# Where the factors of the RMS norms are multiplied in: a ten-sublayer kernel on one core

## The chip, the core and the metric

The kernel runs on one core of one Trainium2 chip. The metric is the device time of one execution in microseconds (us), the median of several. The core's engines each work through their own list of instructions in order: TensorE (PE in the profile; its weight loads are PEld), VectorE (DVE), ScalarE (ACT), GpSimd (POOL) and SyncE (SP), which here issues the transfers. An instruction starts when what stands before it on its engine is done and what it reads and writes is ready on the others.

## The reference, cut to what matters

256 tokens of width 1024 pass through ten sublayers, all in float32. Each one normalises its input, computes something from it, normalises the result and adds it to x:

```
def rms_norm(x, w):
    y = x * rsqrt(mean(x * x, -1) + 1e-6)
    return y * w

for l in range(2):
    x = x + 0.5 * rms_norm(swiglu(rms_norm(x, pre0)), post0)        # (l, 0)
    x = x + rms_norm(mixer(rms_norm(x, pre1)), post1)               # (l, 1)
    x = x + rms_norm(cross_attention(rms_norm(x, pre2)), post2)     # (l, 2)
    x = x + 0.5 * rms_norm(swiglu(rms_norm(x, pre3)), post3)        # (l, 3)
x = x + rms_norm(mixer2(rms_norm(x, pre)), post)                    # (2, 0)
x = x + rms_norm(square(relu(rms_norm(x, pre) @ w1)) @ w2, post)    # (2, 1)

swiglu(u) = (silu(u @ w_gate) * (u @ w_up)) @ w_down                # 1024 -> 2816 -> 1024
```

The mean in the norm makes one number per token, called the factor here: x is multiplied by the factor and by a weight per column. The two mixers of the first block hold a gated delta rule, whose triangular systems are solved in levels (the inverse stage below), a retention and a short convolution; `mixer2` has four groups of its own. Their formulas don't matter for what follows.

## The kernel before, in words

x lies in SBUF for the whole time, as two tiles of 128 tokens (tile 0 and 1) in one long table, named `tables` in the rows. All products take their operands as two float32 numbers of reduced length, a high half (h) and a low half (l), and are three matmuls each: high by high, low by high, high by low (`mm3`, at L436). The weights come as units of 512 KB. SP transfers a unit into one of three `raw` buffers, ScalarE casts it to the high half `wh` (L393), and VectorE subtracts to get the low half `wl` (L394; POOL does so for some units). A raw buffer is free for the next transfer when both have read it.

A sublayer boundary, for each token tile, is this chain:

- `post` (L498 to L512): ScalarE squares the two result banks with a running sum (L502), POOL makes the factor in three instructions (the sum of both halves at L504, scale and epsilon at L453, the power -1/2 at L456), VectorE multiplies each bank by factor and weight into `pd` (L510) and adds `pd` to x (L512).
- `normT` (L483 to L496), the pre-norm of the next sublayer: the same Squares on x (L488), the same three POOL instructions (L490, L453, L456), then VectorE makes `u` = x * factor * weight, in two halves of 512 columns (L495).
- `toT`: TensorE transposes `u` into a PSUM bank (L439), ScalarE casts the bank to `xh` (L393) and VectorE subtracts to get `xl` (L394). Now the next sublayer's products can read the tile.

While this chain runs for one tile, TensorE works on the other tile's products where there are any.

A feed-forward sublayer (`ffn`) goes through its 2816 hidden columns in blocks, a first one of 256 (`wh` tiles then hold four of the eight contraction steps of a projection) and five of 512. For each block and token tile: gate product, up product, Silu of the gate (L611), its product with the up result into `hf` (L613), transposes of `hf`, down product into banks that stay for the whole sublayer. The MLP (`mlp`, (2, 1)) has eight blocks of 512 with the Relu of L1924 in their place.

The order of instructions on each engine is not the order of the code. A planner lays the whole program out beforehand on a simulated timeline and fixes one order per engine; a change of some instructions can move others anywhere. At the start, x's first tile comes first, then a 128 x 128 unit matrix, the weight of the first pre-norm, the first weight unit and x's second tile.

## Time and profile before

| | us |
|---|---|
| median of 3 runs | 1839.99 |
| the three runs | 1834.03, 1839.99, 1847.09 |
| the profiled execution: its time | 1836.08 |
| its span in the trace | 1834.0 |

[...] Busy times in the span: TensorE 1768.2 us, its weight loads 1517.9 (they run beside matmuls), VectorE 1077.6, ScalarE 908.2, POOL 201.9. The busy time of an engine is the sum over its instructions without overlap; where a row says `[1.94 <-DVE u L495]`, the engine stood idle for 1.94 us before this instruction, and what it waited for last was `u` of line 495 on VectorE. A row with x2 stands for two instructions one after the other, with the time of both.

### The profile page before, as it was taken

To read this page: it belongs to the slowest core of one execution; us is meant where nothing else is said; L and a number is where in the kernel's file an instruction comes from. 1 tells how busy PE (TensorE), PEld (TensorE's weight loads), DVE (VectorE), ACT (ScalarE), POOL (GpSimd) and SP (SyncE) were. 2 spreads that over 40 slices of the span, in tenths; PEclk is the share of its full clock that TensorE was granted. 3 is DMA by queue.
4 is the path that set the end of the run, shared out by engine and by line. 5 is a ranking of instruction groups with operands and counts; after the bars stand their busy time and mean duration, and the time that the engine had idled before them with its cause. 6 is when DMAs were issued, how large, how long until landed. Compare 5 with 4: busy or idle time off the path is not lost. (4 is left out here: it accounts for less than half of the span.)

```text
span 1834.0 us, 25097 instructions
## 1 busy us (share of the span) xinstructions
PE 1768.2 (96%) x9712; PEld 1517.9 (83%) x9712; DVE 1077.6 (59%) x1544; ACT 908.2 (50%) x1458; POOL 201.9 (11%) x240
## 2 busy tenths in 40 slices
PE   7999999999999999999999999999999899989998
PEld 6888799888988887888789988988888788878886
DVE  5454577765555546555467676546455668465554
ACT  5434565545544445444465464545344676344442
POOL 0000343121000000000133211000000120110000
PEclk9999999999999999999999999999999999599999
DMA  7555432434536664656544332636567532135552
GB/s 250 207 200 198 155 130 76 132 96 146 162 137 197 197 197 143 207 185 202 187 144 138 96 115 84 206 122 205 164 196 219 170 135 76 39 126 173 187 177 84
DMA packets 82775, 287.05 MB, mean 157 GB/s; under 512 B 11104, under 2 KB 12512, under 8 KB 82656
## 3 DMA queue, kind: packets, MB, share of 16 engines
q1 hardware_dynamic: 82656, 285.46, 47.9%
q8 instruction: 76, 1.25, 0.3%
q14 instruction: 43, 0.35, 0.1%
HBM read 284.37 MB, written 1.05 MB: 156 GB/s over the span
## 5 line engine op out<-in xcount | busy, mean ns | idle before, releaser
L394 DVE TENSOR_TENSOR wl<-raw,wh 128x1024 fp32r<-128x1024 f32 x473 | 576.6, 1231 | 361.3 <-ACT wh L393 323.6
L393 ACT CAST wh<-raw 128x1024 fp32r<-128x1024 f32 x505 | 521.1, 1051 | 339.8 <-DMA raw<-in_wst 196.3
L436 PE MATMUL mm<-wh,xh 128*128 128x512 f32 (+1 forms) x1184 | 457.7, 388 | 6.4 <-ACT xh L393 6.1
L436 PE MATMUL mm<-wh,xl 128*128 128x512 f32 (+1 forms) x1184 | 452.5, 385 | 8.7 <-DVE xl L394 8.6
L436 PE MATMUL mm<-wl,xh 128*128 128x512 f32 (+1 forms) x1184 | 453.1, 384 | 0.3 <-DVE wl L394 0.3
L436 PEld LDWEIGHTS mm<-wh,xl 128*128 128x128 f32 x1184 | 225.2, 191 | 55.0 <-DVE xl L394 12.8
L436 PEld LDWEIGHTS mm<-wh,xh 128*128 128x128 f32 x1184 | 226.0, 191 | 51.2 <-ACT xh L393 10.2
L436 PEld LDWEIGHTS mm<-wl,xh 128*128 128x128 f32 x1184 | 225.7, 191 | 41.3 <-DVE wl L394 1.1
L436 PE MATMUL bank<-wh,xh 128*128 128x512 f32 x544 | 213.3, 392 | 4.4 <-ACT xh L393 4.4
L436 PE MATMUL bank<-wl,xh 128*128 128x512 f32 x544 | 213.8, 393 | 0.0
L436 PE MATMUL bank<-wh,xl 128*128 128x512 f32 x544 | 201.7, 390 | 0.0
L436 PE MATMUL mm<-xh,wh 128*128 128x256 f32 x552 | 160.1, 290 | 0.0
L436 PE MATMUL mm<-xh,wl 128*128 128x256 f32 x552 | 158.5, 288 | 0.7 <-DVE wl L394 0.6
L436 PE MATMUL mm<-xl,wh 128*128 128x256 f32 x552 | 158.7, 288 | 0.0
L394 DVE TENSOR_TENSOR xl<-tr,xh 128x512 fp32r<-128x512 f32 (+1 forms) x118 | 77.2, 664 | 108.0 <-ACT xh L393 107.8
L394 POOL TENSOR_TENSOR wl<-raw,wh 128x1024 fp32r<-128x1024 f32 x32 | 84.7, 2649 | 458.5 <-ACT wh L393 451.9
L393 ACT CAST xh<-tr 128x512 fp32r<-128x512 f32 (+1 forms) x118 | 65.9, 565 | 135.3 <-PE tr L439 134.4
L436 PEld LDWEIGHTS bank<-wh,xh 128*128 128x128 f32 x544 | 102.1, 188 | 28.0 <-ACT xh L393 6.4
L436 PEld LDWEIGHTS bank<-wh,xl 128*128 128x128 f32 x544 | 102.2, 188 | 21.1
L436 PEld LDWEIGHTS bank<-wl,xh 128*128 128x128 f32 x544 | 102.2, 188 | 20.5
L436 PEld LDWEIGHTS mm<-xh,wl 128*128 128x128 f32 x552 | 106.7, 194 | 2.2 <-DVE wl L394 1.5
L436 PEld LDWEIGHTS mm<-xh,wh 128*128 128x128 f32 x552 | 106.9, 194 | 1.4 <-issue 0.7
(458 smaller groups left out, 2004.5 us busy)
## 6 DMA issues: line engine op xcount, KB each, us to landing
raw<-in_wst SPq DMA_DIRECT2D x505, 512.0 KB, 4.4
wpre<-in_norm_pre SPq DMA_DIRECT2D x8, 512.0 KB, 6.5
wpost<-in_norm_post SPq DMA_DIRECT2D x8, 512.0 KB, 6.1
mem<-in_mem SPq DMA_DIRECT2D x4, 512.0 KB, 3.4
rel<-in_rel SPq DMA_DIRECT2D x2, 512.0 KB, 4.4
wmem<-in_mem_norm SPq DMA_DIRECT2D x2, 512.0 KB, 3.8
out<-tables SPq DMA_DIRECT2D x4, 256.0 KB, 2.1
abias<-in_abias SPq DMA_DIRECT2D x3, 256.0 KB, 4.1
```

The source lines that it names most:

```text
L393: a = self.nc.scalar.copy(h, raw)
L394: return a, (eng or self.nc.vector).tensor_tensor(out=l, in0=raw, in1=h.bitcast(F32), op=ALU.subtract)
L436: return self.place(self.nc.tensor.matmul(out, a, b, start=start, stop=stop))
```

## The change

The three POOL instructions of a factor become two (`mean_rsqrt`): the scale moves into ScalarE's Squares, sum and epsilon become one instruction, the power stays. In `post`, each bank is multiplied by its weight right behind the Squares, without the factor (`pd`), and factor and addition become one instruction, x = pd * factor + x. In `normT` a norm may be late: then `u` = x * weight without the factor, the transposes follow, and the Squares and the factor come behind them. Since the factor is one number per token, and a product's row belongs to one token, it can be multiplied into the product's result. The late norms are the pre-norms of the four feed-forward sublayers and of the MLP, whose first products are read in one place each: the Silu takes the factor as its scale, `hf` = up * factor * silu; the MLP's Relu takes the factor's square as its scale, r2, made once for each tile. The other five pre-norms multiply the factor in at `u`, as before. `tables` has 32 more columns, for the factors that now live longer.

```diff
+    def mean_rsqrt(self, halves, f, out=None, then=None):
+        ss = self.small(2, "ss")
+        for g in range(2):
+            nc.scalar.activation(self.junk, halves[g], AF.Square, scale=math.sqrt(f / DM), accum_out=ss[:, g:g + 1])
+            if then:
+                then(g)
+        s1 = self.small(1, "s1")
+        nc.gpsimd.tensor_scalar(out=s1, in0=ss[:, 1:2], scalar1=ss[:, 0:1], scalar2=f * EPS, op0=ALU.add, op1=ALU.add)
+        r = self.small(1, "rs") if out is None else out
+        nc.gpsimd.tensor_tensor(out=r, in0=s1, in1=self.mhalf, op=ALU.pow)
+        return r
...
-    def normT(self, src, wb, T, t):
+    def normT(self, src, wb, T, t, late=None):
...
+        if late is None:
+            rs = self.mean_rsqrt(halves, 1.0)
         for g in range(2):
...
-            nc.vector.scalar_tensor_tensor(out=u, in0=src[:, sl], scalar=rs, in1=wb[:, sl], op0=ALU.mult, op1=ALU.mult)
+            if late is None:
+                nc.vector.scalar_tensor_tensor(out=u, in0=halves[g], scalar=rs, in1=w, op0=ALU.mult, op1=ALU.mult)
+            else:
+                nc.vector.tensor_tensor(out=u, in0=halves[g], in1=w, op=ALU.mult)
             self.toT(u, T, g * 4, 4, t)
+        if late is not None:
+            self.mean_rsqrt(halves, 1.0, late)
...
     def post(self, t, banks, wb, half):
...
+        def then(g):
+            d = self.w("pd")
+            nc.vector.tensor_tensor(out=d, in0=banks[g], in1=wb[:, g * 512:g * 512 + 512], op=ALU.mult)
+            ds.append(d)
+        rs = self.mean_rsqrt(banks, 4.0 if half else 1.0, None, then)
         for g in range(2):
-            nc.scalar.activation(self.junk, banks[g], AF.Square, accum_out=ss[:, g:g + 1])
...
-            nc.vector.scalar_tensor_tensor(out=d, in0=banks[g], scalar=rs, in1=wb[:, sl], op0=ALU.mult, op1=ALU.mult)
-            xg = self.x[t][:, sl]
-            nc.vector.tensor_tensor(out=xg, in0=xg, in1=d, op=ALU.add)
+            xg = self.x[t][:, g * 512:g * 512 + 512]
+            nc.vector.scalar_tensor_tensor(out=xg, in0=ds[g], scalar=rs, in1=xg, op0=ALU.mult, op1=ALU.add)
...
-            nc.scalar.activation(s_[:, :fw], pg[:, :fw], AF.Silu)
+            nc.scalar.activation(s_[:, :fw], pg[:, :fw], AF.Silu, scale=rs[t])
             h = self.w("hf")
-            nc.vector.tensor_tensor(out=h[:, :fw], in0=pu[:, :fw], in1=s_[:, :fw], op=ALU.mult)
+            nc.vector.scalar_tensor_tensor(out=h[:, :fw], in0=pu[:, :fw], scalar=rs[t], in1=s_[:, :fw], op0=ALU.mult, op1=ALU.mult)
...
+                if j == 0:
+                    nc.vector.tensor_tensor(out=r2[t], in0=rs[t], in1=rs[t], op=ALU.mult)
                 r_ = self.w("relu")
-                nc.scalar.activation(r_, ps, AF.Relu)
+                nc.scalar.activation(r_, ps, AF.Relu, scale=r2[t])
...
+        late = lambda l, s: (l, s) == (2, 1) or l < 2 and s in (0, 3)
```

The lines of the changed kernel are numbered otherwise: L502 and L488 become one line, L488; L510 becomes L521, L512 becomes L526, `u` without factor is L509, the Silu L625, the square of the factor L1939. How the planner's order moves is shown at three places.

At the start of the program, TensorE, before. Numbers behind a name tell the buffers apart. The bank `mm_237` is the up product of tile 0, whose second half of the contraction reads `xh_109`; `mm_273` is the gate product of tile 1, which reads the second tile's part of `xh_108`.

```order
L436 MATMUL mm_237<-wh_178,xl_110 128x256
L436 MATMUL mm_237<-wh_184,xh_109 128x256
L436 MATMUL mm_273<-wh_103,xh_108 128x256
L436 MATMUL mm_273<-wl_104,xh_108 128x256
L436 MATMUL mm_237<-wl_185,xh_109 128x256
L436 MATMUL mm_237<-wh_184,xl_111 128x256
```

The same place in the change, where the up product is `mm_231` and tile 1's gate product `mm_267`:

```order
L436 MATMUL mm_231<-wh_178,xl_111 128x256
L436 MATMUL mm_231<-wh_178,xh_109 128x256
L436 MATMUL mm_231<-wl_179,xh_109 128x256
L436 MATMUL mm_231<-wh_178,xl_111 128x256
L436 MATMUL mm_267<-wh_103,xh_108 128x256
L436 MATMUL mm_267<-wl_104,xh_108 128x256
```

All twelve matmuls of the up product's second half now stand ahead of tile 1's first gate product; before, eleven of them stood behind its first two.

ScalarE at the same place, before; the last two `xh` casts are those of tile 1, and `sg` is the Silu of tile 0:

```order
L393 CAST wh<-raw 128x1024 x2
L393 CAST rtile<-wab 128x128
L861 ACTIVATE tables<-tables 128x8 x2
L393 CAST wh<-raw 128x1024
L611 ACT_TABLE_LOAD
L611 ACTIVATE sg<-mm 128x256
L393 CAST wh<-raw 128x1024
L393 CAST xh<-tr 128x4x128 x2
L393 CAST wh<-raw 128x1024 x3
L611 ACTIVATE sg<-mm 128x256
```

And in the change, behind the last `xh` cast of tile 0:

```order
L488 ACTIVATE tables,ss<-tables 128x512
L393 CAST wh<-raw 128x1024
L393 CAST xh<-tr 128x4x128
L393 CAST wh<-raw 128x1024
L393 CAST rtile<-wab 128x128
L875 ACTIVATE tables<-tables 128x8 x2
L393 CAST wh<-raw 128x1024
L393 CAST xh<-tr 128x4x128
L393 CAST wh<-raw 128x1024
L625 ACT_TABLE_LOAD
L625 ACTIVATE sg<-mm,tables 128x256
L393 CAST wh<-raw 128x1024 x3
```

The two `xh` casts of tile 1 now stand apart, three weight casts and one weight cast sooner and both ahead of the Silu; the Silu stands behind one more weight cast.

VectorE at the boundary from the second mixer to the MLP, before. `pd<-tr` belongs to tile 0, `pd<-mm` to tile 1:

```order
L394 TENSOR_TENSOR xl<-bank,xh 128x2x128
L510 SCALAR_TENSOR_TENSOR pd<-tr,rs_14666,wpost 128x512 x2
L512 TENSOR_TENSOR tables<-tables,pd 128x512 x2
L495 SCALAR_TENSOR_TENSOR u<-tables,rs_14685,wpre 128x512 x2
L510 SCALAR_TENSOR_TENSOR pd<-mm,rs_14724,wpost 128x512 x2
L394 TENSOR_TENSOR xl<-tr,xh 128x4x128
L512 TENSOR_TENSOR tables<-tables,pd 128x512
L394 TENSOR_TENSOR xl<-tr,xh 128x4x128
L512 TENSOR_TENSOR tables<-tables,pd 128x512
L394 TENSOR_TENSOR wl<-raw,wh 128x1024 x3
```

And in the change:

```order
L521 TENSOR_TENSOR pd<-tr,wpost 128x512 x2
L394 TENSOR_TENSOR xl<-bank,xh 128x2x128
L526 SCALAR_TENSOR_TENSOR tables<-pd,rs,tables 128x512 x2
L509 TENSOR_TENSOR u<-tables,wpre 128x512 x2
L1939 TENSOR_TENSOR tables<-tables 128x1
L521 TENSOR_TENSOR pd<-mm,wpost 128x512 x2
L394 TENSOR_TENSOR xl<-tr,xh 128x4x128
L526 SCALAR_TENSOR_TENSOR tables<-pd,rs,tables 128x512 x2
L394 TENSOR_TENSOR xl<-tr,xh 128x4x128
L509 TENSOR_TENSOR u<-tables,wpre 128x512
L394 TENSOR_TENSOR wl<-raw,wh 128x1024
```

The products with the post weight stand ahead of the `xl` of their surroundings, the additions behind it; `u` of tile 0 follows its x directly, with the square of the factor (L1939) behind it.

VectorE in the inverse stage of the first mixer, before. `P1s` and `X` are the steps of the level chain (L711, L716, which become L725 and L730), `conv` the convolution's steps (L892, which become L906):

```order
L394 TENSOR_TENSOR wl<-raw,wh 128x1024
L711 TENSOR_TENSOR P1s<-P_2467,tables 128x512
L711 TENSOR_TENSOR P1s<-P_2497,tables 128x512
L394 TENSOR_TENSOR wl<-raw,wh 128x1024
L716 TENSOR_TENSOR X<-X,P_2549 128x128x4
L892 SCALAR_TENSOR_TENSOR conv<-st,tables,conv 128x254
L716 TENSOR_TENSOR X<-X,P_2572 128x128x4
```

And in the change:

```order
L725 TENSOR_TENSOR P1s<-P_2483,tables 128x512
L906 SCALAR_TENSOR_TENSOR conv<-st,tables,conv 128x254
L913 SCALAR_TENSOR_TENSOR conv<-th,conv 128x512
L906 SCALAR_TENSOR_TENSOR conv<-st,tables,conv 128x254
L730 TENSOR_TENSOR X<-X,P_2535 128x128x4
L906 SCALAR_TENSOR_TENSOR conv<-st,tables,conv 128x255
L730 TENSOR_TENSOR X<-X,P_2558 128x128x4
```

Steps of the convolution now stand between the steps of the chain where weight splits stood, here and at the same place of the second layer.

## Rows read from the trace of the kernel before

**Rows 1.** Page, busy time of TensorE and the others, share, instructions:

```profile
PE 1768.2 (96%) x9712; PEld 1517.9 (83%) x9712; DVE 1077.6 (59%) x1544; ACT 908.2 (50%) x1458; POOL 201.9 (11%) x240
```

**Rows 2.** TensorE's waits by releaser: total us, number of waits, longest.

```profile
PE tr L439 <- DVE u L495: 19.8, 11, 8.8
PE mm L436 <- DVE xl L394: 8.6, 7, 1.6
PE mm L436 <- ACT xh L393: 6.1, 6, 3.5
```

**Rows 3.** Timeline, second mixer to MLP: start us, us, engine, line, operation, idle before.

```profile
1627.03 0.19 POOL L504 TENSOR_TENSOR s<-ss 128x1 f32<-128x1 f32 x1 [5.51 <-ACT tables L502]
...
1627.59 0.56 POOL L456 TENSOR_TENSOR rs<-rs,tables 128x1 f32<-128x1 f32 x1
...
1628.18 1.41 DVE L510 SCALAR_TENSOR_TENSOR pd<-tr,rs,wpost 128x512 f32<-128x512 f32 x2 [0.51 <-POOL rs L456]
...
1629.51 1.28 DVE L512 TENSOR_TENSOR tables<-tables,pd 128x512 f32<-128x512 f32 x2
...
1630.28 0.63 ACT L488 ACTIVATE tables<-tables 128x512 bf16<-128x512 f32 x1 [3.07 <-DVE tables L512]
...
1632.39 0.56 POOL L456 TENSOR_TENSOR rs<-rs,tables 128x1 f32<-128x1 f32 x1
...
1632.99 1.41 DVE L495 SCALAR_TENSOR_TENSOR u<-tables,rs,wpre 128x512 f32<-128x512 f32 x2 [2.19 <-POOL rs L456]
...
1633.88 1.29 PE L439 MATMUL tr<-tables,u 128*128 128x128 f32 x8 [1.94 <-DVE u L495]
...
1635.12 1.41 DVE L510 SCALAR_TENSOR_TENSOR pd<-mm,rs,wpost 128x512 f32<-128x512 f32 x2 [0.72 <-POOL rs L456]
...
1635.19 0.50 PE L436 MATMUL mm<-wh,xh 128*128 128x512 f32 x1
...
1637.18 0.79 PE L436 MATMUL mm<-wh,xl 128*128 128x512 f32 x1 [1.16 <-DVE xl L394]
```

**Rows 4.** Timelines of ScalarE and of TensorE at the start.

```profile
17.91 1.05 ACT L393 CAST wh<-raw 128x1024 fp32r<-128x1024 f32 x1 [3.21 <-DMA raw<-in_wst]
...
21.88 1.04 ACT L393 CAST wh<-raw 128x1024 fp32r<-128x1024 f32 x1 [1.23 <-DMA raw<-in_wst]
22.84 1.06 ACT L393 CAST xh<-tr 128x512 fp32r<-128x512 f32 x2
...
19.67 0.28 PE L436 MATMUL mm<-wh,xh 128*128 128x256 f32 x1
23.47 0.39 PE L436 MATMUL mm<-wh,xh 128*128 128x256 f32 x1 [3.52 <-ACT xh L393]
```

**Rows 5.** Timeline of the end.

```profile
1828.35 1.41 DVE L510 SCALAR_TENSOR_TENSOR pd<-bank,rs,wpost 128x512 f32<-128x512 f32 x2 [4.48 <-POOL rs L456]
1829.68 1.28 DVE L512 TENSOR_TENSOR tables<-tables,pd 128x512 f32<-128x512 f32 x2
```

**Rows 6.** Windows, busy us (x instructions) of five engines, granted clock, DMA share, GB/s.

```profile
211.00:217.00 6.00, 5.35 (x16) 4.25 (x17) 6.00 (x6) 3.27 (x6) 2.85 (x2) 0.72 0.00 0
...
1635.00:1643.00 8.00, 6.83 (x19) 4.87 (x18) 7.21 (x9) 4.90 (x9) 2.82 (x4) 0.57 0.23 71
1430.00:1446.00 16.00, 11.79 (x53) 8.46 (x53) 14.48 (x37) 11.47 (x20) 4.29 (x7) 1.00 0.37 131
...
1550.00:1610.00 60.00, 56.46 (x280) 50.79 (x279) 34.28 (x85) 21.58 (x57) 7.85 (x10) 0.60 0.12 40
```

**Rows 7.** Groups by line and form: busy us, mean ns of one.

```profile
L495 DVE SCALAR_TENSOR_TENSOR u<-tables,rs,wpre 128x512 f32<-128x512 f32 x40 | 28.3, 748 | 31.2 <-POOL rs L456 31.2
...
L613 DVE TENSOR_TENSOR hf<-mm,sg 128x512 f32<-128x512 f32 x40 | 27.3, 684 | 13.5 <-PE mm L436 13.5
...
L887 ACT ACTIVATE conv<-st,tables 128x256 f32<-128x256 f32 x24 | 12.3, 511 | 0.5
...
L886 ACT COPY st<-mm 128x256 f32<-128x256 f32 x24 | 8.9, 373 | 21.6 <-PE mm L436 19.3 <-issue 2.3
```

More of the change, by code (lines that the diff above doesn't have):

```diff
@@ L287, in __init__ @@
         nc = self.nc
-        self.tables, self.used = self.cst.tile([128, 5744], F32, name="tables"), 0
+        self.tables, self.used = self.cst.tile([128, 5776], F32, name="tables"), 0
         self.x = []
@@ L487, in normT @@
         for g in range(2):
-            nc.scalar.activation(self.junk, src[:, g * 512:g * 512 + 512], AF.Square, accum_out=ss[:, g:g + 1])
+            nc.scalar.activation(self.junk, halves[g], AF.Square, scale=math.sqrt(f / DM), accum_out=ss[:, g:g + 1])
+            if then:
+                then(g)
         s1 = self.small(1, "s1")
-        nc.gpsimd.tensor_tensor(out=s1, in0=ss[:, 0:1], in1=ss[:, 1:2], op=ALU.add)
-        rs = self.rsqrt(s1, 1.0 / DM, EPS)
+        nc.gpsimd.tensor_scalar(out=s1, in0=ss[:, 1:2], scalar1=ss[:, 0:1], scalar2=f * EPS, op0=ALU.add, op1=ALU.add)
@@ L496, in normT @@
             self.toT(u, T, g * 4, 4, t)
+        if late is not None:
+            self.mean_rsqrt(halves, 1.0, late)
     def post(self, t, banks, wb, half):
         nc = self.nc
-        ss = self.small(2, "ss2")
-        for g in range(2):
-            nc.scalar.activation(self.junk, banks[g], AF.Square, accum_out=ss[:, g:g + 1])
-        s1 = self.small(1, "s1")
-        nc.gpsimd.tensor_tensor(out=s1, in0=ss[:, 0:1], in1=ss[:, 1:2], op=ALU.add)
-        f = 4.0 if half else 1.0
-        rs = self.rsqrt(s1, f / DM, f * EPS)
@@ L507, in post @@
-        for g in range(2):
-            d = self.w("pd")
-            sl = slice(g * 512, g * 512 + 512)
-            nc.vector.scalar_tensor_tensor(out=d, in0=banks[g], scalar=rs, in1=wb[:, sl], op0=ALU.mult, op1=ALU.mult)
-            xg = self.x[t][:, sl]
-            nc.vector.tensor_tensor(out=xg, in0=xg, in1=d, op=ALU.add)
+        ds = []
+        def then(g):
+            d = self.w("pd")
+            nc.vector.tensor_tensor(out=d, in0=banks[g], in1=wb[:, g * 512:g * 512 + 512], op=ALU.mult)
+            ds.append(d)
@@ L598, in ffn_plan, with ffn @@
             self.plan((nm + "_down", l, j), fw // 128)
-    def ffn(self, l, s, T, wpost, after):
+    def ffn(self, l, s, T, wpost, after, rs):
         nc = self.nc
@@ L1909, in mlp_plan, with mlp @@
             self.plan(("mlp2", j), 4)
-    def mlp(self, T, wpost, after):
+    def mlp(self, T, wpost, after, rs):
         nc = self.nc
         self.mark("mlp")
+        r2 = [self.tab(1), self.tab(1)]
         accs = [[self.bank() for g in range(2)] for t in range(2)]
@@ L1975, in run @@
         T = self.newT()
+        rs = [self.tab(1), self.tab(1)]
         for t in range(2):
-            self.normT(self.x[t], wp, T, t)
+            self.normT(self.x[t], wp, T, t, rs[t] if late(*subs[0]) else None)
         self.tri = None
@@ L1984, in run @@
                 self.mix2_tables()
-            nT = []
+            nT, nrs = [], [self.tab(1), self.tab(1)]
             bw = {}
@@ L1994, in run, with after @@
             if i + 1 < len(subs):
-                def after(t, bw=bw, nT=nT, nl=subs[i + 1]):
+                def after(t, bw=bw, nT=nT, nl=subs[i + 1], nrs=nrs):
                     if t == 0:
                         nT.extend(self.newT())
-                    self.normT(self.x[t], bw["pre"], nT, t)
+                    self.normT(self.x[t], bw["pre"], nT, t, nrs[t] if late(*nl) else None)
                     if t == (nl in FB):
@@ L2005, in run @@
             if l == 2:
-                (self.mix2 if s == 0 else self.mlp)(T, po, after)
+                if s == 0:
+                    self.mix2(T, po, after)
+                else:
+                    self.mlp(T, po, after, rs)
             elif s == 0 or s == 3:
-                self.ffn(l, 1 if s == 0 else 2, T, po, after)
+                self.ffn(l, 1 if s == 0 else 2, T, po, after, rs)
             elif s == 1:
@@ L2012, in run @@
                 self.xattn(l, T, kv, po, after)
-            T = nT
+            T, rs = nT, nrs
 def kernel(**inputs):
```

4 lines of the change are left out of this document (3 added, 1 removed).

## The prediction

> **What bounds the kernel now.** I read the busy shares first: TensorE is busy for 1768.2 of 1834.0 us and no other engine reaches 60% [rows 1]. So a change can only pay where TensorE stands still or runs at half clock, and the next view is TensorE's list of waits. Its largest entries belong to the norms. Transposes waited for the normalised tile `u` 19.8 us in 11 places, of which one, 8.8 us, is the start of the program; the other ten are sublayer boundaries and make 11.0 us. First products waited 8.6 us in seven places for `xl`, the low half of the transposed tile. They waited 6.1 us for `xh`, the high half, of which 3.5 in one place [rows 2]. Third, the timeline of one boundary (second mixer to MLP, 1626 to 1638 us) shows what lies in these waits: one chain over four engines. The Pool factor (three instructions, 1627.03 to 1628.15), two multiplies and two adds on VectorE (1628.18 to 1630.79), two Squares on ScalarE from 1630.28, a second Pool factor (ready at 1632.95), then `u` at 1632.99; the transposes start at 1633.88 after 1.94 us of idleness. The first products then wait 1.16 us more, because VectorE computes the second token tile's `pd` (1.41 us from 1635.12) before it gets to `xl` [rows 3].
>
> **The change, part by part.** The time of the profiled execution is 1836.1 us, 3.9 under the median of the runs shown; the sum is made against 1836.1.
>
> *Boundary chain.* Pool's first instruction starts 0.56 us before its third (1627.03 and 1627.59); of the two steps in between one goes, so 0.28 us per factor [rows 3]. In `post`, the product with the weight moves ahead of the factor; behind it stand two fused multiply-adds. The nearest row is `u`, which is fused too and reads both its tiles from SBUF: 1.41 us for two, 0.75 one alone [rows 3, 7]. The first half of x is then ready 0.75 us after the factor. Now it takes until 1630.2, which is 2.0 us, since both multiplies run before the first add [rows 3]. The second weight product waits behind the second Square of its bank and behind `xl` work on VectorE; I take 0.3 us back for that. An ordinary boundary chain is thus 0.28 + 1.25 + 0.28 - 0.3 = 1.5 us shorter. Where the following norm is a late one, `u` follows x at once: two fused operations (1.41) and a plain product (0.68, [rows 7]), 2.1 us after the factor. Now this is 1628.15 to 1633.75, 5.6 us [rows 3]. So 5.6 - 2.1 + 0.28 - 0.3 = 3.5 us shorter.
>
> *(a) Waits for u, 11.0 us in ten places.* Their mean is 1.1 us, below 1.5; the 1.94 stands at a late place, below 3.5. For the first token tile they should vanish. For the second tile the chain starts only after TensorE's last product, and TensorE arrives sooner by what it has gained before. I leave 2.0 us there and take **9.0** (bounds: half, 5.0; all, 11.0).
>
> *(b) Waits for xl, 8.6 us in seven places.* VectorE's row order now has the weight products before `xl` and the adds behind it, as the quoted VectorE rows show. `xl` then follows `xh` by one operation of 0.68 us, of which the two products with `xh` that come first (0.50 the one at 1635.19) cover most [rows 3]. The mean of the seven is 1.2 us; I count on five of them at 1.0 each, less 0.2 where the products have 256 columns and cover less, and leave two to weight splits that may still stand ahead: **4.8** (bounds: half of that, 2.5, and seven at 1.0, 7.0).
>
> *(c) The start.* ScalarE's queue holds a weight cast that waits 1.23 us for its transfer until 21.88; behind it stand the two `xh` casts of the second token tile, and TensorE waits 3.52 us for them [rows 4]. In the new order, as quoted, one of these casts stands ahead of the weight cast of 17.91, the other right behind it: both done at 17.91 + 1.05 + 0.53 = 19.5. TensorE asks for them later than now, when it comes to a stop behind the product of 19.67: the twelve products of the up product's second half now stand first [rows 4]. So the 3.52 us go. But the Silu now stands behind the late weight cast, and what hangs on it may come late; I take 0.5 back: **3.0** (bounds 0, if that cast binds again, and 3.5).
>
> *(d) The end.* The last two multiplies and adds take from 1828.35 to 1830.96 [rows 5]; two fused operations take 1.41, so 1.20, and one Pool instruction, 0.28: **1.5** (bounds 1.2 and 1.5).
>
> *(e) The clock.* Behind three boundaries the granted clock is 0.72 over 6 us twice (211 to 217 and 918 to 924, of which the first is shown) and 0.57 over 8 us: 1.7 + 1.7 + 3.4 = 6.8 us lost, since at half clock a product takes twice as long. Another boundary had 4.2 us of idle in 16 and stayed at 1.00 [rows 6], so idleness alone does not decide. I take a little over a third, **2.5** (bounds 0 and 6.8). [...]
>
> *What is added.* 48 Silus and 16 Relus get their scale as a per-token column. The nearest rows are the convolution's activation with two such columns (511 ns) and a copy of the same shape (373 ns) [rows 7]: 0.07 us per column, 4.5 us of ScalarE in all. [...] The 48 `hf` products become fused ones, 0.75 for 0.68, 3 us of VectorE. Two 128x1 squares of the factor come in the MLP. The late Squares and their factor now run behind `u`; the Silu that reads the factor comes a whole projection later. All of it costs nothing on the path, because ScalarE is half idle and waits for TensorE before these; without that cover at most 7.5 us would come back.
>
> Sum: 9.0 + 4.8 + 3.0 + 1.5 + 2.5 = **20.8 us**, bounds 8.7 and 29.8. 1836.1 - 20.8 = 1815.3; from the median, 1819.2. I say **1817 us**.
>
> **The rivals.**
>
> *Half of it turns into another wait (21%).* At some boundaries ScalarE's order keeps a weight cast, which waits for a transfer, ahead of the second tile's Square or of its `xh`. For this speaks the start, where exactly such a cast held TensorE [rows 4]; against it, that the transfers are released by VectorE's splits, which come earlier too. Then (a) gives 5, (b) 4, (c) 0, (d) 1.5, (e) 0: 10.5 us, 1826.
>
> *The clock holds as well (13%).* All of (e), and the upper ends of (a) and (b) in part: 25 to 30 us, 1808. The half-clock stretches behind boundaries speak for it [rows 6], the 16 us stretch against.
>
> *The planner's new order loses the clock in the two first mixers (9%).* The change makes the scheduler lay out the whole program anew; in both layers' inverse stage, convolutions move between the steps of the level chain, as quoted. What such a stage can cost shows the later mixer's: granted clock 0.60 over 60 us with TensorE busy for 56.5, so 24 us lost [rows 6]. If both layers fell that far, 48 - 20.8 = 27 us slower than now, 1863. A loss of 20.8 cancels the gain, so one layer alone; slower by over 1% it is from 43 (1858.4 - 1836.1 + 20.8). Against it: TensorE's rows in these stages are the same products, and it did not wait there.
>
> *It does not do what it says (8%).* The factor is needed anyway; if Silu, Relu or VectorE's square waits for the late one, the wait only moves. In the MLP's place, as quoted, that square stands ahead of the second tile's weight products. The late factor takes half of x (0.75) and the stretch from the first Square to the end of Pool (1630.28 to 1632.95, 2.67) less the dropped step (0.28): 3.1 us behind the post factor, against 2.8 for both `u` (1.41 + 2 x 0.68). So VectorE stands for 0.3 us at one place [rows 3]; this smallness speaks against it; a ScalarE that comes late to those Squares would speak for it. Time: 1836.
>
> **How the numbers follow.** The forecast has 49%. A measurement of this kernel can tell about 1% from no change: under 1821.6 is faster, over 1858.4 slower, from the median of 1840.0. The forecast's own spread, by its bounds, puts 39 of its 49 under 1821.6. Faster: 39 + 13 + 2 of the first rival = 54%. Same: 10 + 19 + 8 = 37%. Slower: 9%. For the range I go from 1836.1 - 29.8, and a few us of spread between executions (the runs shown differ by 13 us), to the case with nothing gained from the profile's side: 1801 to 1834.
>
> **What would show it.** In the profile of the changed kernel the waits of transposes for `u` without the start should fall from 11.0 to about 2 us; the products' waits for `xl` from 8.6 to about 4. The 3.52 us wait near 23.5 us should be gone, with no new one before 30 us. The last factor to the end of the last multiply-add should take 1.4 us instead of 2.6. The granted clock behind the three boundaries tells (e). The forecast is wrong if TensorE's idle sum falls by less than 10 us, if new waits for `xh` of over 1 us stand behind weight casts, or if the first two mixers' inverse stages fall to the 0.60 of the later one.

## The result

The changed kernel takes 1816.78 us (median of 4 runs, 1815.29 to 1825.88), the kernel before 1838.79 in the same series: ratio 0.9886, 95% interval 0.9837 to 0.9935. In a second series of five rounds the ratio was 0.9879 (0.9841 to 0.9917). The forecast was 1817, so the total came out. Two of its five terms, the waits for `u` and the clock, did not.

Page of the changed kernel, first line and part 1, against [rows 1]:

```profile
span 1814.8 us, 25159 instructions
...
PE 1756.1 (97%) x9712; PEld 1510.9 (83%) x9712; DVE 1088.4 (60%) x1546; ACT 921.0 (51%) x1458; POOL 208.5 (11%) x196
```

TensorE's idle time fell from 1834.0 - 1768.2 = 65.8 us to 58.7, by only 7.1 of the 19.2 us that the span lost. The other 12.1 us are busy time: the same 9712 instructions took less of it. At most 7.8 of them are the clock, of which these two executions lost 45.9 and 38.1 us (next section); the rest, some 4 us, is neither a wait that the profile shows nor clock, and stays open. By the prediction's own last sentence (an idle sum that falls by less than 10) its path was wrong although its sum was right.

TensorE's waits of the changed kernel (total us, number, longest), against [rows 2]:

```profile
PE tr L439 <- DMA tables<-in_ident: 8.6, 1, 8.6
PE tr L439 <- DVE u L507: 6.5, 3, 2.5
PE mm L436 <- ACT xh L393: 4.7, 8, 1.2
...
PE ab L436 <- ACT xh L393: 2.4, 2, 1.3
...
PE tr L439 <- DVE hf L627: 1.5, 2, 1.2
...
PE mm L436 <- DVE xl L394: 1.4, 2, 1.2
...
PE tr L439 <- DVE h L1943: 0.9, 1, 0.9
```

No `u` of a late norm (L509) is waited for any more: of the first transposes the list now names the unit matrix, not `u`. The waits for `xl` fell from 8.6 to 1.4. But the norms that are not late (L507) still make 6.5 us in three places, and the waits for `xh` away from the start grew from 6.1 - 3.5 = 2.6 to 4.7 + 2.4 = 7.1. The wait for `hf` is new.

The boundary into the MLP, timeline of the changed kernel, against [rows 3]:

```profile
1614.56 0.30 POOL L492 TENSOR_SCALAR s<-ss 128x1 f32<-128x1 f32 x1 [5.54 <-ACT tables L488]
...
1615.54 1.41 DVE L526 SCALAR_TENSOR_TENSOR tables<-pd,rs,tables 128x512 f32<-128x512 f32 x2
...
1616.87 1.29 DVE L509 TENSOR_TENSOR u<-tables,wpre 128x512 f32<-128x512 f32 x2
...
1619.27 1.04 PE L439 MATMUL tr<-tables,u 128*128 128x128 f32 x8
...
1620.74 0.50 PE L436 MATMUL mm<-wh,xh 128*128 128x512 f32 x1 [0.43 <-ACT xh L393]
1620.85 0.68 DVE L394 TENSOR_TENSOR xl<-tr,xh 128x512 fp32r<-128x512 f32 x1
```

From POOL's sum to `u` it is 2.31 us where it was 5.96 (1627.03 to 1632.99): 3.65 shorter, 3.5 forecast. `u` is ready at 1618.2, before TensorE is free for it, and `xl` follows `xh` at once.

### The profile page after: what moved, and what is told of

It is laid out like the page before. It is cut to its first block, busy times and chain, and to the rows that moved or that the text cites. A ratio compares the mean times of both kernels' runs of the same rounds, so it can differ in the third digit from the quotient of the medians.

```text
span 1814.8 us, 25159 instructions
## 1 busy us (share of the span) xinstructions
PE 1756.1 (97%) x9712; PEld 1510.9 (83%) x9712; DVE 1088.4 (60%) x1546; ACT 921.0 (51%) x1458; POOL 208.5 (11%) x196
## 4 chain that ended last, share of the span: by engine, by line
PE 83%; DVE 6%; ACT 4%; DMA 2%; issue 2%; POOL 1%; DVEq 0%; POOLq 0%; ACTq 0%
PE mm L436 48%; PE bank L436 21%; DMA raw<-in_wst 2%; PE tr L439 2%; PE P L436 2%; DVE wl L394 1%; PE tr L436 1%; PE tp L439 1%; ACT wh L393 1%; PE hs L436 1%; DVE conv L906 1%; PE oT L436 1%; PE sc L436 1%; ACT tables L488 1%; PE R L436 1%
## 5 line engine op out<-in xcount | busy, mean ns | idle before, releaser
L394 DVE TENSOR_TENSOR wl<-raw,wh 128x1024 fp32r<-128x1024 f32 x473 | 584.2, 1240 | 426.5 <-ACT wh L393 394.5
L393 ACT CAST wh<-raw 128x1024 fp32r<-128x1024 f32 x505 | 526.5, 1051 | 411.0 <-DMA raw<-in_wst 290.3
L394 POOL TENSOR_TENSOR wl<-raw,wh 128x1024 fp32r<-128x1024 f32 x32 | 90.0, 2813 | 473.6 <-ACT wh L393 459.1
L492 POOL TENSOR_SCALAR s<-ss 128x1 f32<-128x1 f32 x44 | 25.6, 582 | 850.2 <-ACT tables L488 850.0
L436 PEld LDWEIGHTS mm<-xl,wh 128*128 128x128 f32 x552 | 107.2, 194 | 0.9 <-issue 0.3
```

The costliest lines, as they stand in the source:

```text
L393: a = self.nc.scalar.copy(h, raw)
L394: return a, (eng or self.nc.vector).tensor_tensor(out=l, in0=raw, in1=h.bitcast(F32), op=ALU.subtract)
L436: return self.place(self.nc.tensor.matmul(out, a, b, start=start, stop=stop))
L492: nc.gpsimd.tensor_scalar(out=s1, in0=ss[:, 1:2], scalar1=ss[:, 0:1], scalar2=f * EPS, op0=ALU.add, op1=ALU.add)
```

## Two numbers for every execution

Every timed execution lists its span and its mean granted clock. The span times one minus the clock is called the time lost to half clock here; the span times the clock is what would be left if TensorE always had the full clock and nothing else changed. Over all executions of all series (means; in brackets the standard error; the clock has three digits, 1.8 us a step):

| kernel | executions | span | lost to half clock | span x clock |
|---|---|---|---|---|
| before | 61 | 1841.1 | 53.7 (0.7) | 1787.5 (0.3) |
| two-step factor alone | 12 | 1835.3 | 52.0 (1.4) | 1783.3 (0.6) |
| new post (and two-step factor) | 6 | 1829.4 | 48.2 (1.1) | 1781.2 (0.8) |
| late norms alone | 6 | 1827.4 | 44.5 (1.5) | 1782.9 (1.0) |
| changed, two late norms | 6 | 1821.8 | 44.3 (1.7) | 1777.4 (1.0) |
| **changed** | 10 | 1817.4 | 40.7 (1.8) | 1776.7 (0.9) |

The change is 23.7 us of mean span: 10.8 in span x clock and 13.0 of clock. And the spread of one kernel's executions is nearly all clock: before loses 36.6 to 66.7 us to it from execution to execution, while its span x clock scatters by 2.4 (standard deviation). The profile on which the prediction was made had 45.9 lost (1834.0 x 0.025), 8 less than the mean. Its line by core, and two windows of 1 us that show the two levels of the granted clock here, 0.50 and 1.00 of full speed (the third number from the end):

```profile
core 0: 1834.0 us, clock 0.975
...
1640.00:1641.00 1.00, 1.00 (x4) 0.81 (x3) 1.00 (x2) 0.01 (x1) 0.91 (x1) 0.50 0.03 8
1643.00:1644.00 1.00, 1.00 (x6) 0.84 (x5) 0.96 (x2) 0.00 (x0) 0.01 (x1) 1.00 1.00 303
```

The split is not exact. Among the 61 executions of before, the span grows by 0.73 us (standard error 0.04) for each us more of lost time, not by 1. So span x clock takes off too much: by this slope about 9.5 of the 23.7 us are the clock's and about 14 the rest. The numbers below are the plain products.

## The experiments

Ratios are against runs of the kernel before on the same chip. Theory A in what was written ahead is that the chains at the boundaries got shorter, place by place; B that the planner's new layout and the clock did it.

**The new post alone** (no norm late; `post` and `mean_rsqrt` as changed):

```diff
-                    self.normT(self.x[t], bw["pre"], nT, t, nrs[t] if late(*nl) else None)
+                    self.normT(self.x[t], bw["pre"], nT, t)
...
-            nc.scalar.activation(s_[:, :fw], pg[:, :fw], AF.Silu, scale=rs[t])
+            nc.scalar.activation(s_[:, :fw], pg[:, :fw], AF.Silu)
```

> No norm is late: only post has the new order (weight product ahead of the factor, fused multiply-add behind it), and every factor takes two POOL instructions instead of three. Theory A, that the gain is made of shorter chains at the boundaries, place by place: the tail keeps its gain (1.4 us from the last factor to the end), the boundaries that were not late in the full change gain what they gained there (about 4 us together), the late ones get the ordinary 1.0 to 1.5 us each; the start keeps its 3.5 us wait. Together 8 to 9 us of the 19, so about 1829 beside a before of 1838. Theory B, that the time comes from the planner's new layout and from the clock granted in it, not from the chains: no relation to the parts; the waits of the transposes for u fall, but the time lies anywhere within 10 us of before, with the half-clock stretches at other places than in either kernel.

Measured: ratio 0.9934 (0.9911 to 0.9957); 6.3 us of span x clock, 5.5 of clock, together more than the 8 to 9 that A gave. And the wait of 3.5 us at the start did not stay: its profile has no wait for `xh` of over 1.1 us (more on this at the two-step factor).

**The late norms alone** (`post` and the three-step factor as before):

```diff
-            nc.vector.tensor_tensor(out=d, in0=banks[g], in1=wb[:, g * 512:g * 512 + 512], op=ALU.mult)
+            nc.vector.scalar_tensor_tensor(out=d, in0=banks[g], scalar=rs, in1=wb[:, sl], op0=ALU.mult, op1=ALU.mult)
...
-            nc.vector.scalar_tensor_tensor(out=xg, in0=ds[g], scalar=rs, in1=xg, op0=ALU.mult, op1=ALU.add)
+            nc.vector.tensor_tensor(out=xg, in0=xg, in1=d, op=ALU.add)
```

> Only the late norms: u without the factor for the five feed-forward pre-norms, the factor in Silu, hf and Relu; post and the factor with its three POOL instructions as in the kernel before. Theory A: the start gives 3 to 4.4 us, the boundary into the MLP 3 to 4, the three boundaries into a feed-forward sublayer about 1 each; the tail takes 2.6 us from the last factor as before. Together about 10 us, so 1828 beside 1838. If the two parts add up, the gains of this run and of the run with the new post alone make 17 to 20 us. Theory B: the two don't add up by more than 8 us, and the difference is found in half-clock time.

Measured: 0.9926 (0.9901 to 0.9951); 4.6 us of span x clock, 9.2 of clock, more than the 10 that A gave. The two parts add up: 6.3 + 4.6 = 10.9 beside 10.8 for both, in clock 5.5 + 9.2 = 14.7 beside 13.0. TensorE's idle sums do not: 0.6 us less with the new post alone (1831.4 - 1766.2 = 65.2), 3.5 less with the late norms alone (1827.2 - 1764.8 = 62.4), 7.1 less with both. Their busy times and waits (of the new post alone, then of the late norms alone) show what each part removes; in the second, L505 are the norms that are not late and L507 the late ones:

```profile
PE 1766.2 (96%) x9712; PEld 1521.3 (83%) x9712; DVE 1089.7 (60%) x1544; ACT 912.2 (50%) x1458; POOL 200.4 (11%) x196
```

```profile
PE tr L439 <- DVE u L507: 23.5, 8, 9.1
...
PE mm L436 <- DVE xl L394: 2.0, 3, 1.1
```

```profile
PE 1764.8 (97%) x9712; PEld 1517.7 (83%) x9712; DVE 1082.0 (59%) x1546; ACT 921.2 (50%) x1458; POOL 200.7 (11%) x240
```

```profile
PE tr L439 <- DVE u L505: 9.4, 6, 2.6
...
PE mm L436 <- DVE xl L394: 5.5, 5, 1.6
...
PE tr L439 <- DVE u L507: 3.9, 4, 1.1
```

The new post takes the waits for `xl` away (2.0 are left of 8.6), the late norms alone leave 5.5. For `u`, neither alone does anything: 23.5 - 9.1 (the start) = 14.4 us and 9.4 + 3.9 = 13.3, beside 11.0 before. Where `xl` is no longer waited for, TensorE seems to be only sooner at the next `u`. With both it is 6.5. The new post alone also has two new waits of 2.73 us in the level chains of the first block's mixers, at 279 and 984 us, where neither before nor the changed kernel waits longer than 1.2: a sign of the planner's layout.

**The two-step factor alone:**

```diff
-        rs = self.rsqrt(s1, f / DM, f * EPS)   # three POOL instructions; pd and x as before
+        rs = self.mean_rsqrt(banks, 4.0 if half else 1.0)
```

> Only the factor in two POOL instructions instead of three, with the scale in the Squares; both products and the addition in the order before. Theory A: 0.28 us at each wait for u or at the end, about 10 of them: 2 to 3 us, 1835 beside 1838. Theory B: an edit of this kind makes the planner lay out the program anew, so the time can differ by 5 us or more in either direction, in half-clock stretches that have nothing to do with the factor.

Measured: 0.9967 (0.9950 to 0.9984), 4.2 us of span x clock and 1.7 of clock (standard error 1.5): a real gain, and twice the 2 to 3 us that A gives. Its profile speaks against A as the reason, since the waits for `u` without the start are not shorter (21.3 - 8.8 = 12.5, before 11.0):

```profile
PE tr L439 <- DVE u L507: 21.3, 12, 8.8
```

What did change is the start, where nothing of the edit aims. One of the two `xh` casts of tile 1 now stands ahead of the late weight cast, and the wait of 3.52 us is gone; a wait for `hf` stands in its place:

```profile
16.32 0.59 ACT L393 CAST xh<-tr 128x512 fp32r<-128x512 f32 x1 [1.03 <-PE tr L439]
...
26.89 0.45 PE L439 MATMUL tr<-tables,hf 128*128 128x128 f32 x2 [2.08 <-DVE hf L623]
```

TensorE's hundredth instruction starts 2.3 us sooner than before (28.2 and 30.5), 1.7 of it a half-clock stretch that before has at 24 to 28 us (mean granted clock 0.57). The whole difference is 5.9 us, the size that B had named, though not mainly in half-clock time; the start shows a part of it as layout, the rest was not found. And the wait of 3.52 us goes with any of these edits: it hangs on the planner's order and not on the late norm.

**No weight split on POOL:**

```diff
-POOLED = ("w_in",)
+POOLED = ()
```

> The changed kernel, but the 32 weight splits that POOL did go to VectorE too. At the two boundaries into a first-block mixer the changed kernel's transposes wait 2.5 us for u, because the 128x1 sum on POOL took 2.2 us beside a VectorE split and stood behind POOL's own split of 2.4 us. Theory A1, that POOL's own split and VectorE's splits beside it hold the factor: the wait for u falls to about 1 us or less at both boundaries and the VectorE splits there take 1.2 us instead of 3.3: 3 us faster, 1814 beside 1817. Rival A2, that only VectorE's splits lock POOL out: the sum still takes over 1 us, the wait falls by less than 1 us. Rival A3: VectorE, now with 39 us more of splits in the two input projections, makes TensorE wait for wl there, 5 us or more slower.

Measured: 1.0012 (0.9987 to 1.0037), the whole gain gone. At the two boundaries the wait for `u` fell by 0.92 and 0.83 us, to 1.55 and 1.63, and the sum still took 1.38 us at the first of them, which is A2's sign; the splits beside it took 1.16 each, which is A1's. But A3 won, at a place that it did not name:

```profile
PE bank L439 <- DVE y L1157: 9.6, 2, 5.0
...
PE tr L439 <- DVE u L507: 5.2, 4, 1.6
```

```profile
210.59 1.38 POOL L492 TENSOR_SCALAR s<-ss 128x1 f32<-128x1 f32 x1 [4.24 <-ACT tables L488]
```

VectorE reaches `y`, at the end of each mixer, 5 us late; against the changed kernel 10.7 us of span x clock and 15.8 of clock went.

**Both kernels once more:**

> The changed kernel once more, nothing edited, timed in the same series as the others. Theory A (gain of 12 us from waits and 7 us of granted clock, the latter a property of the instruction order): the profile shows the same half-clock stretches within one or two (37 us lost in sum, 35 to 40), and a ratio of 0.986 to 0.990. Theory B (the clock's share is luck of one execution): the sum of half-clock time differs by 5 us or more from the first profile.

> The kernel before once more, nothing edited, for a second profile. Theory A: its half-clock stretches are the same, 44 us lost in sum within 3, and its waits are the same within 0.5 us. Theory B: 5 us or more of half-clock time more or less than in the first profile, so that single profiles cannot carry the clock's share of the gain.

The changed kernel's second profile lost 1814.9 x 0.020 = 36.3 us to half clock beside 38.1; the kernel before 49.6 beside 45.9. For the changed kernel A holds. For before the difference is 3.7, between the two theories' bounds, and its waits differ by more than A's 0.5 us: 8.6 and 7.8 for `xl`, 6.1 and 7.8 for `xh`. So a single profile tells a sum of waits to a us or two, and not the clock's share.

**Fewer POOL splits.** First without block 7 of w_in, then without 7 and 5:

```diff
-        pooled = key[0] in POOLED and self.nfetch % POOLN == 0
+        pooled = key[0] in POOLED and key[2] not in (7, 5) and self.nfetch % POOLN == 0
```

> The changed kernel, but POOL splits none of the first four weight units of a first-block mixer (w_in block 7), which are split beside the boundary; the other units of w_in as before, so VectorE gets 4 splits more, not 32. Theory A1 (POOL's own split and its contention hold the factor at this boundary, and the loss with no POOL split at all came from later in the mixer): the wait for u at both boundaries falls from 2.5 to about 1.5 us and no waits of 5 us for y appear at the mixers' ends; 2 to 4 us faster, 1814 beside 1817. Rival A3 (VectorE has no room there): waits for xl or wl behind the boundary take it back, 0 to 2 us slower.

> The changed kernel, but POOL splits no unit of the first two w_in blocks of a first-block mixer (7 and 5). The run that kept only block 7 off POOL left the split beside the boundary where it was, since units are fetched ahead: it belonged to block 5. Theory A1: without POOL's own split beside it the sum on POOL takes 1.4 us instead of 2.2 and starts up to 0.3 us sooner, the VectorE split beside it 1.2 instead of 3.3; the wait for u at both boundaries falls from 2.5 to 1.5 us, with no waits of 5 us at the mixers' ends. Without half-clock time the span should be 2 to 3 us shorter than the changed kernel's 1777; with it, it can come out anywhere within 10 us, since the layout behind the boundary changes too. Rival A3: waits for xl or wl take it back.

The first (0.9867, 0.9829 to 0.9906) left the boundary as it was: units are fetched ahead, and the split beside the factor belonged to block 5. The second tells what stood there. Its ratio is 0.9869 (0.9847 to 0.9892), its span x clock 1775.9 (1.0). The boundary into the first mixer, timeline of the changed kernel:

```profile
207.13 2.40 POOL L394 TENSOR_TENSOR wl<-raw,wh 128x1024 fp32r<-128x1024 f32 x1 [1.89 <-ACT wh L393]
...
207.36 4.40 DVE L394 TENSOR_TENSOR wl<-raw,wh 128x1024 fp32r<-128x1024 f32 x2
...
209.63 2.21 POOL L492 TENSOR_SCALAR s<-ss 128x1 f32<-128x1 f32 x1
...
212.52 1.42 DVE L507 SCALAR_TENSOR_TENSOR u<-tables,rs,wpre 128x512 f32<-128x512 f32 x2 [0.76 <-POOL rs L494]
213.32 1.32 PE L439 MATMUL tr<-tables,u 128*128 128x128 f32 x8 [2.47 <-DVE u L507]
...
214.17 1.04 ACT L393 CAST wh<-raw 128x1024 fp32r<-128x1024 f32 x1 [2.68 <-DMA raw<-in_wst]
215.12 1.07 ACT L393 CAST xh<-tr 128x512 fp32r<-128x512 f32 x2
...
215.76 0.29 PE L436 MATMUL ab<-xh,rtile 128*16 128x256 f32 x1 [1.11 <-ACT xh L393]
```

and of the kernel without POOL splits in blocks 7 and 5:

```profile
205.94 3.48 DVE L394 TENSOR_TENSOR wl<-raw,wh 128x1024 fp32r<-128x1024 f32 x3
208.05 1.46 POOL L492 TENSOR_SCALAR s<-ss 128x1 f32<-128x1 f32 x1 [4.24 <-ACT tables L488]
...
210.99 1.32 PE L439 MATMUL tr<-tables,u 128*128 128x128 f32 x8 [1.56 <-DVE u L507]
```

The sum of one column takes 0.30 us alone, 2.21 beside VectorE's splits, and two of these take 4.40 with POOL's split beside them, three 3.48 without. Both hold each other up, and the trace shows how for POOL. Of the 44 sums of the changed kernel, 15 took longer than 0.31 us; every one of them ran beside a split or a `u`, which read two tiles in SBUF, and ended 0.08 to 0.17 us behind the end of the last of these. The other 29 took 0.30 or 0.31 us, alone or beside `pd` and `xl`, which read a PSUM bank (one overlapped the end of a `u`). So each of the 15 was held until VectorE's run of such instructions was over, one to three of them here.

In the changed kernel a second wait stands at the place: the `xh` cast is behind a weight cast that had waited for its transfer, 1.11 us, as the first rival had it. In the second kernel it is gone, but 0.74 us for `xl` stands instead. So A1 holds at the waits for `u`, which fell by 0.9 us, and 0.8 us (standard error 1.3) of span x clock is no gain that a timing shows.

**The sum on VectorE:**

```diff
-        nc.gpsimd.tensor_scalar(out=s1, in0=ss[:, 1:2], scalar1=ss[:, 0:1], ...
+        nc.vector.tensor_scalar(out=s1, in0=ss[:, 1:2], scalar1=ss[:, 0:1], ...
```

> The changed kernel, but the sum of the two halves and epsilon, POOL's first instruction of each factor, is done by VectorE; the power stays on POOL. Theory A2 (a 128x1 instruction of POOL takes 1 to 2.7 us where VectorE splits weights beside it, 0.31 otherwise): on VectorE it takes 0.2 us, but stands behind a split in its order; the power, which now starts earlier, is held instead where a split runs beside it. The mean of the sum falls from 582 to about 200 ns, the wait for u at the two first-block mixers from 2.5 to 1.5 us, the time by 0 to 3 us. If the long times were the profile's rough spans on POOL and not a hold, nothing changes at these boundaries but 0.1 to 0.3 us.

Measured: 0.9929 (0.9905 to 0.9952), slower than the changed kernel by 5.4 us of span x clock and 4.9 of clock, against the expectation: the waits for `u` at these boundaries are 2.64 us. That is the change of 0.1 to 0.3 us that a mere fault of POOL's spans in the profile would give, but it can't tell, as the sum now stands in VectorE's own order behind the same two splits (4.57 us here). The run only shows that this way round is no better; for the hold speak the ends of the 15 sums above.

**Fillers in the second mixer:**

```diff
+                rec = nc.vector.reciprocal(rc[:, :n], sm[:, :n])   # as before, now named
...
+                if hs == (0, 2):
+                    for _ in range(14):
+                        self.order_after(self.mm(ps[:, :384], self.identr, self.rtile[:, 256:640]), rec)
                 self.transposes(ps, S, 4)
```

> The changed kernel with 14 matmuls of 384 columns more, whose results nobody reads: they write the PSUM bank that the next transposes overwrite, and stand in TensorE's order at the one place in the second mixer where the transposes wait 2.5 us for the softmax tile S, just ahead of a stretch of 45 us at half clock (22 us lost). TensorE's order up to there is the same row by row. Theory C (the clock is lost where TensorE comes to a stand of 2 to 3 us, and in this stage, of short matmuls, it stays lost): with the stand filled the granted clock stays at 1.00 through much of the stretch: 10 to 22 us faster, 1795 to 1807 beside 1817. Rival C1 (the short, serial matmuls of the stage lose the clock whatever stands ahead): the stretch starts within 5 us of where it did, the time is the same or up to 2 us longer for the fillers.

Measured: 0.9859 (0.9833 to 0.9884), lost to half clock 37.5 (2.4), the changed kernel 40.7 (1.8): no difference that holds. Windows of this kernel (busy us of TensorE and the others, granted clock, DMA share, GB/s), and the row of the fillers:

```profile
1536.00:1546.00 10.00, 9.26 (x73) 8.04 (x72) 9.03 (x18) 6.57 (x12) 0.96 (x1) 1.00 0.01 2
1546.00:1554.00 8.00, 7.97 (x34) 7.42 (x35) 7.08 (x14) 3.58 (x9) 0.00 (x0) 0.57 0.27 79
1554.00:1560.00 6.00, 4.76 (x34) 4.13 (x34) 2.66 (x8) 2.31 (x7) 0.96 (x1) 1.00 0.30 114
1560.00:1595.00 35.00, 35.00 (x159) 32.38 (x159) 16.14 (x42) 11.14 (x36) 6.08 (x8) 0.51 0.00 0
```

```profile
1550.97 3.92 PE L436 MATMUL tr<-rtile 128*128 128x384 f32 x14
```

A clock of 0.57 over 8 us is 6.9 us at the lower level, so it fell by 1547.1 at the latest, before the fillers came at 1550.97; the longest wait of TensorE in the 25 us ahead of the fillers is 0.82 us. It stood at 1.00 for 6 us behind them and fell again at about 1560, where the profile shows TensorE busy without a pause (it models where a matmul ends, so short pauses can hide). Theory C, that a stand of 2 to 3 us loses the clock here, falls; C1 fits. What in these matmuls loses it stays open.

**Two late norms, the first and the MLP's:**

```diff
-        late = lambda l, s: (l, s) == (2, 1) or l < 2 and s in (0, 3)
+        late = lambda l, s: (l, s) in ((0, 0), (2, 1))
```

> The changed kernel with only two of the five late norms: the first one of the program and the one into the MLP; the three norms into a later feed-forward sublayer take their factor at u again. Over the executions so far, span times mean granted clock is 1787.3 us for the kernel before, 1776.7 for the changed one and 1781.2 for the new post alone, so the late norms bring 4.5 us of it, and another 7.5 of granted clock. Theory D1, from the changed kernel's profile (start 2.5 us, MLP boundary 2.6, at the three others a wait for xh of 1.16 us stands where one for u of 1.5 stood): two late norms bring nearly all of it, span times clock is 1776 to 1778, the time within 4 us of the changed kernel's. Rival D2 (each late norm brings about the same): three fifths are lost again, span times clock 1779 to 1780, time 5 to 8 us longer.

Measured: 0.9904 (0.9881 to 0.9926). Span x clock 1777.4 (1.0), as D1 said: the other three late norms bring little waiting time (0.7 us, standard error 1.3). The waits show why: with two late norms TensorE waits 3.6 us more for `u` (10.1) and 2.8 less for `xh` (1.9). The lost time is 3.6 us higher (standard error 2.5), which is not clear of noise, but the profile shows two pieces that would be part of it. Windows of this kernel and then of the changed one, at the first of the two boundaries from cross-attention (at the second the clock is 0.83 and 1.00 too):

```profile
532.00:542.00 10.00, 8.18 (x53) 7.51 (x52) 7.03 (x9) 6.51 (x10) 0.86 (x2) 0.83 0.25 87
```

```profile
530.00:540.00 10.00, 8.84 (x67) 8.16 (x66) 6.92 (x10) 7.44 (x12) 0.86 (x2) 1.00 0.36 119
```

TensorE stands there for 1.80 and 1.86 us in the first and 1.16 in the second; the first loses 1.7 us of clock on top each time.

**Both edits for a better version** (POOL's splits as in the second edit above, and the unit matrix issued first):

```diff
-        self.ident = self.const("ident", 128)
+        self.first = first = nc.sync.dma_start(self.ident, A["ident"])   # the transfers of x and of the first weight unit are ordered behind it
```

> The changed kernel with two more edits: POOL splits no unit of the first two w_in blocks of a first-block mixer (as measured), and the unit matrix of 64 KB is issued ahead of all other transfers. In the changed kernel the first u is ready at 6.9 us, but the transposes start at 8.59, when that matrix has landed. Theory E1: the first transposes start at 7.0 to 7.5 us and the first product 0.8 to 1.5 us earlier; with 0.8 for POOL's splits, span times clock is 1774 to 1775 beside 1776.7, and the time 2 us shorter than the changed kernel's, which only the profile can show. Rival E2: the first weight unit, the first tile's second half and ScalarE's cast hold the first product at 10.4 us anyway; the transposes start sooner and nothing follows.

Measured: 0.9878 (0.9856 to 0.9900), span x clock 1778.4 (0.6), as the changed kernel. The transposes start at 7.73 us instead of 8.59, the second four at 9.88 (x's second half arrives at 9.14), and the first product at 10.65 (10.36 in the changed kernel), with a wait of 2.61 for `hf` behind: E2. None of these versions is faster than the changed kernel by more than the spread.

## Why the sum was right and its parts were not

*(a) Waits for u, 9.0 forecast.* This step failed. The waits fell by 11.0 - 6.5 = 4.5. Those of the first token tile, seven places and 7.9 us before, are all gone, as forecast. What the step had wrong is the second tile, for which 2.0 us were left: it still waits at the three mixers, whose norms are not late, and there 3.1 us before became 6.5. I had its chain 1.5 us shorter and reckoned with POOL instructions of 0.19 to 0.56 us; held by the splits, the sum alone took 2.21. The rows that were read come from the boundary into the MLP, where nothing held POOL for the first token tile. With a sum of 1.46 us the wait of 2.47 was 1.56, so about 0.9 of it hangs on POOL's own split and the hold; that the rest comes from TensorE arriving sooner is likely and was not shown.

And 4.5 us came as waits for `xh`: 2.4 at the first block's mixers, the rest mostly at the two boundaries behind cross-attention (1.16 each). There no weight cast stands ahead of ScalarE's casts, but the first tile's Silu (0.47 us) with its table load (1.28) and a late Square (0.62), of which the forecast had said that they cost nothing on the path:

```profile
531.14 0.62 ACT L488 ACTIVATE tables<-tables 128x512 bf16<-128x512 f32 x1
...
531.75 1.06 ACT L393 CAST xh<-tr 128x512 fp32r<-128x512 f32 x2
...
532.38 0.39 PE L436 MATMUL mm<-wh,xh 128*128 128x256 f32 x1 [1.16 <-ACT xh L393]
```

*(b) Waits for xl, 4.8.* Mechanism right, size too small: 8.6 - 1.4 = 7.2. The new post alone shows it (2.0 left), as the two-step factor alone leaves 8.7.

*(c) The start, 3.0.* The 3.52 us wait is gone, by the planner's order as forecast; it goes without a late norm too. New waits of 0.72 us (for a weight split) and 1.18 came, the second for the Silu behind the late weight cast, for which I had taken 0.5 back:

```profile
21.36 1.05 ACT L393 CAST wh<-raw 128x1024 fp32r<-128x1024 f32 x1 [3.05 <-DMA raw<-in_wst]
...
23.72 0.47 ACT L625 ACTIVATE sg<-mm,tables 128x256 f32<-128x256 f32 x1
```

TensorE's hundredth instruction starts 4.4 us sooner (30.5 and 26.1), of which 1.7 are the half-clock stretch at 24 to 28 us that I had not read: about 2.7 for the step. The two-step factor alone has 0.5 of it; the rest came only where the first norm was late.

*(d) The end, 1.5.* Right: from the factor to the end 1828.35 to 1830.96 was 2.6 us, now 1.42, and TensorE's last matmul starts 6.7 us before the end instead of 8.1. The dropped POOL instruction brought 0.18 us and not 0.28: the new sum takes 0.30 where the old one took 0.19.

```profile
1810.33 1.42 DVE L526 SCALAR_TENSOR_TENSOR tables<-pd,rs,tables 128x512 f32<-128x512 f32 x2 [0.35 <-POOL rs L494]
```

*(e) The clock, 2.5 with an upper bound of 6.8.* Mis-sized: 13.0 of lost time between the means (standard error 2), about 9.5 us of span by the slope; 7.8 between the two profiles. The bound counted three stretches of one execution that had little lost, and took a product at half clock for twice as long; the rows of before at the MLP's boundary show one of 512 columns every 0.43 us at 0.50 and every 0.23 at 1.00, 1.9 times:

```profile
1640.33 0.63 PE L436 MATMUL mm<-wh,xh 128*128 128x512 f32 x1
1640.76 0.63 PE L436 MATMUL mm<-wl,xh 128*128 128x512 f32 x1
...
1643.63 0.39 PE L436 MATMUL mm<-wl,xh 128*128 128x512 f32 x1
1643.86 0.39 PE L436 MATMUL mm<-wh,xl 128*128 128x512 f32 x1
```

Of the three, the MLP's is gone, the first mixer's stays, the second's grew, so at these places only 6.8 - 5.1 = 1.7 came:

```profile
215.00:221.00 6.00, 5.24 (x23) 3.93 (x24) 1.29 (x2) 1.66 (x4) 2.38 (x1) 0.72 0.45 160
915.00:923.00 8.00, 6.72 (x27) 4.97 (x27) 1.68 (x3) 2.47 (x4) 2.37 (x1) 0.57 0.45 165
1618.00:1630.00 12.00, 10.16 (x51) 7.56 (x50) 9.92 (x16) 9.21 (x17) 5.06 (x6) 1.00 0.26 80
```

What lost the clock at the other places of before, and keeps it now, was not found. That a TensorE with less idle time keeps the higher clock was not shown. For the whole change the two go together, 13.0 us less lost time with 7.1 us less idle time. For the new post alone they don't, 5.5 us (standard error 1.4) with 0.6 less idle time, and the stretch from 1560 us in the filler run, at the lower clock without a pause that the profile shows, is one that idleness does not explain.

So 18.3 us of waits were forecast, and TensorE's idle time fell by 7.1, the span without the lost clock by 10.8; 2.5 of clock were forecast and 13.0 came. That the sum came out all the same is luck. The first rival (waits that return as `xh`, in part behind weight casts) and the second (the clock holds) both happened, with opposite signs. Of the third rival, the planner's layout in the first two mixers, a small part came, as waits and not as clock: TensorE waits 2.4 us there for `P1s`, the level chain's step, in three places where it had not. The rival that the factor is waited for came true once, as 0.9 us: the MLP's second tile waits for `h`, since VectorE stands 0.84 us on the late factor, whose sum took 2.74 us on POOL beside splits (for the first tile it stands 0.85, where 0.3 was reckoned, at no cost):

```profile
1625.49 2.74 POOL L492 TENSOR_SCALAR s<-ss 128x1 f32<-128x1 f32 x1 [4.23 <-ACT tables L488]
```

*What is added.* Groups of the changed kernel (busy us, mean ns):

```profile
L627 DVE SCALAR_TENSOR_TENSOR hf<-mm,tables,sg 128x512 f32<-128x512 f32 x40 | 29.8, 745 | 3.0 <-PE mm L436 2.4
L526 DVE SCALAR_TENSOR_TENSOR tables<-pd,rs,tables 128x512 f32<-128x512 f32 x40 | 28.4, 748 | 3.6 <-POOL rs L494 3.5
...
L509 DVE TENSOR_TENSOR u<-tables,wpre 128x512 f32<-128x512 f32 x20 | 13.1, 686 | 6.7 <-DMA tables<-in_x 6.7
```

```profile
L625 ACT ACTIVATE sg<-mm,tables 128x512 f32<-128x512 f32 x40 | 27.4, 685 | 63.9 <-PE mm L436 63.9
```

The fused operations cost the 0.75 and 0.69 that were read. The Silu went from 594 to 685 ns: 91 per column, not the 70 taken. Here it cost nothing, as ScalarE waits 63.9 us for TensorE there.

## What to carry to other kernels

Split a gain into span x clock and clock before explaining it, over several executions: here a good forecast of the sum hid waits that were 7 us too many and a clock term 10 us too small. Time the smallest part of the change alone too: here it removed the wait at the start as well, which looked like the late norm's work. Price each small instruction of a chain beside what else runs there, not at the one place that was read: POOL's sum took 0.30 us alone and 2.21 beside weight splits. Where a chain waits for a row factor, try it behind the product, and the weight ahead of it, but look for what the freed engine waits for next: here 4.5 us of waits for `u` went and 4.5 came for `xh`.

## What the runs showed of the hardware

POOL's 128x1 sum takes 0.30 us alone or beside VectorE instructions that read a PSUM bank, and 0.68 to 2.74 in the changed kernel where it meets VectorE's weight splits, which read two tiles in SBUF; it then ends 0.08 to 0.17 us behind the last split or `u` beside it. And one unchanged program lost 36.6 to 66.7 us to half clock from execution to execution, of which each us more came with 0.73 us more span.
